# The recurrence's gates as pairs of half-height matmuls

## The chip, the cores and the metric

The kernel runs on one core of a Trainium2 chip. What is compared is the time of one execution in device microseconds (us); for the kernel before it is 1622.69, the median of three runs. The engines are named as in the profile: PE (matmuls) with PEld (its weight loads), DVE (elementwise), ACT (activations by table), POOL and SP (here they mostly issue transfers). SBUF is the memory that the engines work from, with 128 partitions; PSUM holds the matmuls' results, in banks of 128 x 512 numbers.

## The reference

A trunk of two layers over 512 positions with 1024 channels: each layer is a SwiGLU block, a mixer and a second SwiGLU block. The mixer of the first layer is the recurrent one, and only that is changed:

```python
def block_diag_linear(x, w, b):                 # 16 heads of 64 channels
    xh = x.reshape(bsz, s, h, dh)
    return (jnp.einsum('bshi,hij->bshj', xh, w) + b).reshape(bsz, s, h * dh)

def rg_lru(x, w_a, b_a, w_x, b_x, lam):
    gate_a = jax.nn.sigmoid(block_diag_linear(xf, w_a, b_a))
    gate_x = jax.nn.sigmoid(block_diag_linear(xf, w_x, b_x))
    log_a = -LRU_C * gate_a * jax.nn.softplus(-lam)
    a = jnp.exp(log_a)
    mult = jnp.sqrt(-jnp.expm1(2.0 * log_a))
    bx = xf * gate_x * mult
    ...                                         # h[t] = a[t] * h[t-1] + bx[t]

def recurrent_mixer(x, w_in, conv_w, conv_b, ...):
    y, r = jnp.split(x @ w_in, 2, axis=-1)
    r = causal_depthwise_conv(r, conv_w, conv_b)
    return (gelu(y) * rg_lru(r, ...)) @ w_out
```

## The kernel before

The large products are done in blocks of 512 x 512 by a scheme of seven products instead of eight. Every fp32 operand of a product is split into a high and a low part (`split`: ACT makes `hi` by a copy, DVE makes `lo` by a subtraction), and a product is three matmuls, `hi*hi + lo*hi + hi*lo` (`mm3`, L223 to L225).

The work is a list of steps, `subs`. A step is one piece of weight (`raw`, 512 KB, loaded by SP up to eight ahead), its split (`whi` on ACT, `wlo` on DVE, done three steps ahead), and its matmuls. All other work hangs on hooks: `hook(n, phase, fn)` runs `fn` at step `n`, in the phases pre, mid, rest (before the step's matmuls are written down), end and late (behind them). This gives the order in which each engine's instructions stand; each engine takes its own in that order and waits on semaphores for the others'. POOL issues transfers that add a second block of weight to one in SBUF (`raw.add`, L137); it takes its instructions in order too.

In the recurrence (`recurrent`) channels lie on partitions and positions on columns. A group `c` of 128 channels, 0 to 7, is two heads. The input product of `c` gives `r` (a bank of PSUM, 24 matmuls; for c = 0 to 3 the positions come in two halves, because the second half of the normed input is ready later). `r_post(c)` then does, by hooks:

- ACT scales `r` and adds the bias: `rc`. DVE adds the three other taps of the convolution, reading `r` again (`taps`). This ends the use of the bank.
- `rc` is split into `hi` and `lo`.
- `gate`: two block-diagonal weights of 128 x 128, one for a and one for x, each with the two heads' 64 x 64 blocks on the diagonal and zeros elsewhere, give two banks of 128 x 512: 6 matmuls.
- `sigmoids`: ACT makes `g` (a), `g` (x) and from a `tl` (a tanh).
- `product`: DVE multiplies `rc` by the x gate into `pr`.

Behind that come, by `plan`, exponentials of a (groups 0 to 4 together, 5 to 7 together), squares and roots into the factor `tl`, the scan over positions (`scan`), the other half of the input product (y0 to y7, eight more steps), `gelu`, and their product, which is the left side of the output product. The eight banks for products and gates are six (`bank`) in a ring and two others (`aux`). ACT holds one table of functions at a time: sigmoid, exponential, root and gelu each need a load (`ACT_TABLE_LOAD`).

The gates' steps are at `g` = the step of `r` plus 1 or 2, so that gates 3 and 4 follow each other, and 6 and 7.

Of the kernel before, what the change touches and what calls it, by code (L numbers as in the profile page):

```python
# [10 lines left out]
AF = mybir.ActivationFunctionType  # L11
ALU = mybir.AluOpType

P = 128
# [10 lines left out]
V_F1, V_MIX, V_F2, V_CW, V_CB, V_GA, V_GX, V_LAM, V_SB = 0, 16, 32, 48, 80, 88, 96, 104, 112  # L25
# [27 lines left out]
def trunk(ctx: ExitStack, tc: tile.TileContext, a: dict, out: bass.AP):  # L53
    nc = tc.nc
# [12 lines left out]
    def nm(s):  # L67
        uid[0] += 1
        return f"{s}_{uid[0]}"

    def slot(dt=F32, name="s"):
        return sp.tile([P, T], dt, tag="s", name=nm(name))

    def bank(name="ps"):
        return mmp.tile([P, 512], F32, tag="mm", name=nm(name))

    def aux(name="aux"):
        return auxp.tile([P, 512], F32, tag="aux", name=nm(name))
# [4 lines left out]
    def f32(t):  # L83
        return t.bitcast(F32)

    def tt(o, x, y, op):
        nc.vector.tensor_tensor(out=o, in0=x, in1=y, op=op)  # L87
# [4 lines left out]
    def stt(o, x, s, y, op0, op1):  # L92
        nc.vector.scalar_tensor_tensor(out=o, in0=x, scalar=s, in1=y, op0=op0, op1=op1)

    def act(o, x, f, **k):
        nc.scalar.activation(out=o, in_=x, func=f, **k)  # L96

    def split(src):

        w = src.shape[-1]  # L100
        hi, lo = slot(F32R, "hi")[:, :w], slot(F32R, "lo")[:, :w]
        act(hi, src, AF.Copy)
        tt(lo, src, f32(hi), ALU.subtract)
        return hi, lo
# [108 lines left out]
    def hook(n, phase, fn):  # L213


        hooks.setdefault((n, phase), []).append(fn)
# [5 lines left out]
    def mm3(ps, wh, wl, xh, xl, start, stop):  # L222
        nc.tensor.matmul(ps, wh, xh, start=start, stop=False)  # L223
        nc.tensor.matmul(ps, wh, xl, start=False, stop=False)  # L224
        nc.tensor.matmul(ps, wl, xh, start=False, stop=stop)  # L225
# [16 lines left out]
    def vcol(row):  # L242
        return vec[:, row : row + 1]
# [685 lines left out]
    def recurrent(w_in, w_out, norm):  # L929
        gates = {}  # L930

        def load_gates():
            for name in ("a", "x"):
                w = a[f"rec_gate_{name}_w"]
                for q in range(2):
                    g = slot(name="gw")
                    nc.gpsimd.memset(g, 0.0)
                    gv = g.rearrange("p (c j) -> p c j", c=4)
                    wv = w[0, q * 8 : (q + 1) * 8].rearrange("(c two) i j -> two i c j", two=2)
                    for two in range(2):  # L940
                        nc.sync.dma_start(
                            out=gv[two * 64 : (two + 1) * 64, :, two * 64 : (two + 1) * 64], in_=wv[two])
                    gates[name, q] = g

        def split_gate(name, q):
            gates[name, q] = split(gates[name, q])

        at0 = len(subs)
        y0 = at0 + 12
        hook(at0 - 34, "late", load_gates)  # L950
        for n, (name, q) in enumerate((name, q) for q in range(2) for name in ("a", "x")):
            hook(at0 - 26 + 2 * n, "mid", lambda name=name, q=q: split_gate(name, q))

        rc, ga, gx, tl, pr, ym = {}, {}, {}, {}, {}, {}

        def r_post(c, ps):
            n = now[0]
            g = n + (2 if c < 4 or c == 6 else 1)
            v = rc[c] = slot(name="rc")
            hl, pss = [], []  # L960
            act(v, ps, AF.Identity, scale=vcol(V_CW + 24 + c), bias=vcol(V_CB + c))

            def taps():
                for k in (0, 1, 2):
                    stt(v[:, 3 - k :], ps[:, : T - 3 + k], vcol(V_CW + 8 * k + c), v[:, 3 - k :], ALU.mult, ALU.add)

            def gate():
                for name in "ax":
                    pg = bank("gate")
                    wh, wl = gates[name, c // 4]  # L970
                    cs = slice((c % 4) * P, (c % 4 + 1) * P)
                    mm3(pg, wh[:, cs], wl[:, cs], hl[0], hl[1], True, True)
                    pss.append(pg)
                hl.clear()

            def sigmoids():
                for dst, brow in ((ga, V_GA), (gx, V_GX)):
                    dst[c] = slot(name="g")
                    act(dst[c], pss.pop(0), AF.Sigmoid, bias=vcol(brow + c))
                tl[c] = slot(name="tl")  # L980
                act(tl[c], ga[c], AF.Tanh, scale=lru_c[:, c : c + 1])

            def product():
                pr[c] = slot(name="pr")
                tt(pr[c], rc.pop(c), gx.pop(c), ALU.mult)

            hook(n, "late", taps)
            hook(n + 1, "mid", lambda: hl.extend(split(v)))
            hook(g, "end", gate)
            hook(g + 1, "mid", sigmoids)  # L990
            hook(g + 2, "mid", product)

        hh = {}

# [101 lines left out]
        for c in range(4):  # L1096
            again += mk(D + c * P, lambda ps, c=c: r_post(c, ps), True)
        subs.extend(again)
        for c in range(4, KD):
            mk(D + c * P, lambda ps, c=c: r_post(c, ps), False)  # L1100
# [157 lines left out]
    def lru_consts():  # L1258
# [44 lines left out]
        for i in range(13, 0, -2):  # L1303
# [17 lines left out]
    last = FinalNorm()  # L1321
    ffn(a["ffn1_w_in"][0], a["ffn1_w_out"][0], TileNorm(V_MIX))
    recurrent(a["rec_w_in"][0], a["rec_w_out"][0], BlockNorm(V_F2))
    ffn(a["ffn2_w_in"][0], a["ffn2_w_out"][0], BlockNorm(V_F1 + 8))
    ffn(a["ffn1_w_in"][1], a["ffn1_w_out"][1], BlockNorm(V_MIX + 8, True))
# [7 lines left out]

    stage = slot(name="stage")
    rows = [(a["ffn1_norm"], V_F1, 16), (a["mix_norm"], V_MIX, 16), (a["ffn2_norm"], V_F2, 16),
            (a["rec_conv_w"][0], V_CW, 32), (a["rec_conv_b"], V_CB, 8), (a["rec_gate_a_b"], V_GA, 8),
            (a["rec_gate_x_b"], V_GX, 8), (a["rec_lambda"], V_LAM, 8), (a["sg_b_s"][0], V_SB, 8)]
    first_gain = tp.tile([8, P], F32, tag="fgain1", name="first_gain", bufs=1)
    nc.scalar.dma_start(out=first_gain, in_=a["ffn1_norm"][0].rearrange("(n p) -> n p", p=P))

# [33 lines left out]
    ps = aux("vec")  # L1374
# [3 lines left out]
    def vec_rest():  # L1378
        for src, r0, n in rows:
            flat = src.rearrange("h d -> (h d)") if len(src.shape) == 2 else src.rearrange("o h d -> (o h d)")  # L1380
            nc.gpsimd.dma_start(out=stage[r0 : r0 + n, :P], in_=flat.rearrange("(n p) -> n p", p=P))

    def vec_rest_t():
        ps = aux("vec")
        nc.tensor.transpose(ps[:, :V_ROWS], stage[:V_ROWS, :P], ident[:V_ROWS, :V_ROWS])
        opening["vec"] = ps

    first = BlockNorm(V_F1)
# [31 lines left out]
    for n, phase, fn in ((0, "late", vec_rest),  # L1420
                         (2, "pre", lambda: (subs[2].split(True), parts(0, "A11"), parts(1, "A11"))),
                         (2, "pre", lambda: (subs[3].split(), value(0, "A11", True), value(1, "A11", True))),
                         (2, "end", lambda: (turn(0, "A22", bank), turn(1, "A22", bank))),
                         (3, "pre", lambda: (parts(0, "A22"), parts(1, "A22"))),
                         (3, "mid", lambda: (value(0, "A22"), value(1, "A22", True))),
                         (3, "end", lambda: (turn(0, "A21"), turn(1, "A21"))),
                         (4, "mid", lambda: (parts(0, "A21"), parts(1, "A21"))),
                         (4, "rest", lambda: (value(0, "A21"), value(1, "A21")))):
        hook(n, phase, fn)
# [57 lines left out]
```

## Time and profile before

| | |
|---|---|
| median of 3 runs | 1622.69 us (1622.64 to 1623.0) |
| the profiled execution, its own time | 1622.86 us |
| its span in the profile | 1621.2 us |
| PE, DVE, ACT busy | 99%, 85%, 64% of the span |
| the recurrence's input products and gates | about 343 to 445 us of the span |
| all 48 gate matmuls | 366.1 to 407.2 us of the span, with other products between them |

The span runs from the first to the last instruction of one execution; the rows that the prediction shows are of this execution, and their times count from its start.

### The profile page before, as it was taken

To read this page: it belongs to the slowest core of one execution; us is meant where nothing else is said; L and a number is where in the kernel's file an instruction comes from. 1 tells how busy PE (TensorE), PEld (TensorE's weight loads), DVE (VectorE), ACT (ScalarE), POOL (GpSimd) and SP (SyncE) were. 2 spreads that over 40 slices of the span, in tenths; PEclk is the share of its full clock that TensorE was granted. 3 is DMA by queue.
4 is the path that set the end of the run, shared out by engine and by line. 5 is a ranking of instruction groups with operands and counts; after the bars stand their busy time and mean duration, and the time that the engine had idled before them with its cause. 6 is when DMAs were issued, how large, how long until landed. Compare 5 with 4: busy or idle time off the path is not lost.

```text
span 1621.2 us, 20840 instructions
## 1 busy us (share of the span) xinstructions
PE 1608.2 (99%) x7451; PEld 1327.0 (82%) x7451; DVE 1373.8 (85%) x1839; ACT 1036.8 (64%) x1504; POOL 221.8 (14%) x201
## 2 busy tenths in 40 slices
PE   9999999999999999999999999999999999999998
PEld 7888888888888888888888888888888788888886
DVE  6898888888998787877887978878978988879778
ACT  7656556658776556556775565566886766565665
POOL 2111111100010111111101111111211011111110
PEclk9999999999999999999999999999999999999999
DMA  9776876943383786876838768768877557686693
GB/s 275 183 168 166 210 179 158 214 126 105 92 208 86 176 217 156 209 168 158 206 86 192 168 162 212 181 154 208 217 192 191 155 120 192 167 208 159 161 206 100
DMA packets 164695, 279.29 MB, mean 172 GB/s; under 512 B 11520, under 2 KB 38000, under 8 KB 164592
## 3 DMA queue, kind: packets, MB, share of 16 engines
q1 hardware_dynamic: 115088, 184.84, 36.2%
q0 software_dynamic: 47712, 91.30, 33.8%
q10 hardware_dynamic: 1792, 1.84, 0.4%
q8 instruction: 58, 0.95, 0.2%
q14 instruction: 45, 0.37, 0.1%
HBM read 275.84 MB, written 2.10 MB: 171 GB/s over the span
## 4 chain that ended last, share of the span: by engine, by line
PE 94%; DVE 2%; ACT 2%; issue 1%; DMA 0%; SPq 0%; DVEq 0%; ACTq 0%
PE A L365 14%; PE A L366 14%; PE A L367 14%; PE C L366 7%; PE C L367 7%; PE C L365 7%; PE p L751 5%; PE B L365 4%; PE B L367 4%; PE B L366 4%; PE e L265 3%; PE r L225 2%; PE r L223 2%; PE r L224 2%; PE Q L367 1%; PE Q L365 1%
## 5 line engine op out<-in xcount | busy, mean ns | idle before, releaser
L96 ACT ACTIVATE whi<-raw 128x1024 fp32r<-128x1024 f32 (+1 forms) x536 | 553.2, 1033 | 388.0 <-PE A L366 103.9
L87 DVE TENSOR_TENSOR wlo<-raw,whi 128x1024 fp32r<-128x1024 f32 (+1 forms) x537 | 639.7, 1194 | 181.6 <-ACT whi L96 180.3
L365 PE MATMUL A<-whi,hi 128*128 128x512 f32 x1016 | 404.1, 398 | 0.0
L367 PE MATMUL A<-wlo,hi 128*128 128x512 f32 x1016 | 396.9, 391 | 0.0
L366 PE MATMUL A<-whi,lo 128*128 128x512 f32 x1016 | 396.5, 390 | 0.0
L367 PEld LDWEIGHTS A<-wlo,hi 128*128 128x128 f32 x1016 | 190.8, 188 | 41.6 <-DVE wlo L87 0.3
L366 PEld LDWEIGHTS A<-whi,lo 128*128 128x128 f32 x1016 | 191.1, 188 | 38.6 <-DVE lo L87 0.8
L365 PEld LDWEIGHTS A<-whi,hi 128*128 128x128 f32 x1016 | 190.9, 188 | 37.5
L366 PE MATMUL C<-whi,lo 128*128 128x512 f32 x560 | 218.7, 391 | 0.9 <-DVE lo L87 0.8
L365 PE MATMUL C<-whi,hi 128*128 128x512 f32 x560 | 218.5, 390 | 0.0
L367 PE MATMUL C<-wlo,hi 128*128 128x512 f32 x560 | 218.1, 389 | 0.0
L137 POOL DMA_DIRECT2D raw<-in_ffn_w_in_dram x82 | 98.8, 1205 | 741.1 <-DVE raw L87 524.5
L137 POOL DMA_DIRECT2D raw<-in_ffn_w_out_dram x72 | 83.0, 1160 | 378.7 <-DVE wlo L87 148.7
L87 DVE TENSOR_TENSOR raw<-raw,raw 128x1024 f32<-128x1024 f32 (+1 forms) x108 | 129.7, 1201 | 1.1 <-DMA raw<-in_ffn_w_out_dram 0.6
L87 DVE TENSOR_TENSOR lo<-a,hi 128x512 fp32r<-128x512 f32 (+1 forms) x188 | 123.1, 663 | 3.7 <-ACT hi L96 3.3
L366 PEld LDWEIGHTS C<-whi,lo 128*128 128x128 f32 x560 | 105.1, 188 | 24.7 <-DVE lo L87 3.2
L96 ACT ACTIVATE hi<-a 128x512 fp32r<-128x512 f32 (+1 forms) x188 | 112.4, 601 | 17.5 <-DVE a L87 14.3
L365 PEld LDWEIGHTS C<-whi,hi 128*128 128x128 f32 x560 | 105.2, 188 | 21.8
L367 PEld LDWEIGHTS C<-wlo,hi 128*128 128x128 f32 x560 | 105.2, 188 | 21.7
L96 ACT ACTIVATE c<-A 128x512 f32<-128x512 f32 x132 | 77.4, 594 | 56.3 <-PE A L367 55.9
L365 PE MATMUL B<-whi,hi 128*128 128x512 f32 x280 | 112.1, 400 | 0.0
L367 PE MATMUL B<-wlo,hi 128*128 128x512 f32 x280 | 109.4, 391 | 0.0
(161 smaller groups left out, 2106.3 us busy)
## 6 DMA issues: line engine op xcount, KB each, us to landing
raw<-in_ffn_w_in_dram SPq DMA_DIRECT2D x162, 512.0 KB, 4.4
raw<-in_ffn_w_out_dram SPq DMA_DIRECT2D x100, 512.0 KB, 5.3
raw<-in_ffn_w_in_dram POOLq DMA_DIRECT2D x82, 512.0 KB, 7.5
raw<-in_ffn_w_out_dram POOLq DMA_DIRECT2D x60, 512.0 KB, 8.1
raw<-in_sg_w_in_dram SPq DMA_DIRECT2D x20, 512.0 KB, 6.4
raw<-in_rec_w_in_dram SPq DMA_DIRECT2D x16, 512.0 KB, 3.8
raw<-in_ffn_w_in_dram SPq DMA_DIRECT2D x30, 256.0 KB, 5.0
raw<-in_sg_w_in_dram POOLq DMA_DIRECT2D x12, 512.0 KB, 7.8
```

What stands on the lines that cost most here:

```text
L87: nc.vector.tensor_tensor(out=o, in0=x, in1=y, op=op)
L96: nc.scalar.activation(out=o, in_=x, func=f, **k)
L137: nc.gpsimd.dma_start(out=self.v, in_=src, accum_op=ALU.add)
L223: nc.tensor.matmul(ps, wh, xh, start=start, stop=False)
L224: nc.tensor.matmul(ps, wh, xl, start=False, stop=False)
L225: nc.tensor.matmul(ps, wl, xh, start=False, stop=stop)
L265: nc.tensor.transpose(ps[:, o : o + P], src(q, s), ident)
L365: nc.tensor.matmul(ps, zh, wh, start=fresh and i == 0, stop=False, **k)
L366: nc.tensor.matmul(ps, zl, wh, start=False, stop=False, **k)
L367: nc.tensor.matmul(ps, zh, wl, start=False, stop=end, **k)
L751: nc.tensor.matmul(bank_of(half, s), z, (sub.lo if m == 2 else sub.hi)[:, q, :], start=left[2] == "2" and (h, q, m) == (0, 0, 0), stop=lef ...
```

## The change

It does the gates with the two heads apart. A group's weights are now one tile of 128 x 128: in the rows of the first head stand its a columns and then its x columns, in the rows of the second head its x columns and then its a columns, and no zeros. The first head's matmul takes rows 0 to 63 of weight and input, the second's rows 64 to 127, each into a bank of its own, and they are written down in turn: 3 pairs of half-height matmuls per group in place of 6 full ones. The first bank then holds a of the first head above its x, the second x of the second head above its a. So a lies where it belongs, and x is in the other half of the partitions.

The sigmoids' results are put together in one of two ways:

- groups 0, 1, 2 and 5 (`MOVED`): two sigmoids of 128 partitions, and three transfers of 64 x 512 from SBUF to SBUF, issued by POOL: two make the x gate, the third puts the second head's a into its place in `ga`, over what the first transfer reads. The tanh has a hook of its own, later.
- groups 3, 4, 6 and 7: four sigmoids of 64 partitions, which put a in its place, and two transfers for the x gate.

With this the products `pr` of groups 0 to 2 are a step later, gate 5 is a step later (behind r7 instead of r6), the gate weights are two tiles instead of four (two splits less, no clearing by POOL), and the two biases are loaded in four pieces instead of two rows of blocks.

```diff
         def load_gates():
-            for name in ("a", "x"):
-                w = a[f"rec_gate_{name}_w"]
-                for q in range(2):
-                    g = slot(name="gw")
-                    nc.gpsimd.memset(g, 0.0)
-                    gv = g.rearrange("p (c j) -> p c j", c=4)
-                    wv = w[0, q * 8 : (q + 1) * 8].rearrange("(c two) i j -> two i c j", two=2)
-                    for two in range(2):
-                        nc.sync.dma_start(
-                            out=gv[two * 64 : (two + 1) * 64, :, two * 64 : (two + 1) * 64], in_=wv[two])
-                    gates[name, q] = g
+            for q in range(2):
+                g = slot(name="gw")
+                gv = g.rearrange("p (c j) -> p c j", c=4)
+                for two, names in enumerate(("ax", "xa")):
+                    for k, name in enumerate(names):
+                        wv = a[f"rec_gate_{name}_w"][0, q * 8 : (q + 1) * 8].rearrange("(c two) i j -> two i c j", two=2)
+                        nc.sync.dma_start(out=gv[two * H2 : (two + 1) * H2, :, k * H2 : (k + 1) * H2], in_=wv[two])
+                gates[q] = g
...
-        for n, (name, q) in enumerate((name, q) for q in range(2) for name in ("a", "x")):
-            hook(at0 - 26 + 2 * n, "mid", lambda name=name, q=q: split_gate(name, q))
+        for q in range(2):
+            hook(at0 - 24 + 4 * q, "mid", lambda q=q: split_gate(q))
+        HALVES = slice(0, H2), slice(H2, P)
+        MOVED = (0, 1, 2, 5)
 
         def r_post(c, ps):
             n = now[0]
-            g = n + (2 if c < 4 or c == 6 else 1)
+            g = n + (1 if c in (4, 7) else 2)
...
             def gate():
-                for name in "ax":
-                    pg = bank("gate")
-                    wh, wl = gates[name, c // 4]
-                    cs = slice((c % 4) * P, (c % 4 + 1) * P)
-                    mm3(pg, wh[:, cs], wl[:, cs], hl[0], hl[1], True, True)
-                    pss.append(pg)
+                pss.extend(bank("gate") for _ in range(2))
+                w = gates[c // 4]
+                cs = slice((c % 4) * P, (c % 4 + 1) * P)
+                for m in range(3):
+                    for ps, r in zip(pss, HALVES):
+                        nc.tensor.matmul(ps, w[m == 2][r, cs], hl[m == 1][r, :], start=m == 0, stop=m == 2)
                 hl.clear()
 
             def sigmoids():
-                for dst, brow in ((ga, V_GA), (gx, V_GX)):
-                    dst[c] = slot(name="g")
-                    act(dst[c], pss.pop(0), AF.Sigmoid, bias=vcol(brow + c))
+                p0, p1 = pss
+                pss.clear()
+                if c in MOVED:
+                    ga[c], u = slot(name="g"), slot(name="gu")
+                    act(ga[c], p0, AF.Sigmoid, bias=vcol(V_GA + c))
+                    act(u, p1, AF.Sigmoid, bias=vcol(V_GX + c))
+                    swap(c, ga[c][HALVES[1], :], u[HALVES[0], :])
+                    nc.gpsimd.dma_start(out=ga[c][HALVES[1], :], in_=u[HALVES[1], :])
+                    return
+                ga[c], u = slot(name="g"), slot(name="gu")
+                for dst, ps, brow, r in ((ga[c], p0, V_GA, 0), (ga[c], p1, V_GX, 1), (u, p0, V_GA, 1), (u, p1, V_GX, 0)):
+                    r = HALVES[r]
+                    act(dst[r, :], ps[r, :], AF.Sigmoid, bias=vcol(brow + c)[r, :])
+                swap(c, u[HALVES[1], :], u[HALVES[0], :])
+                tanh()
+
+            def swap(c, first, second):
+                gx[c] = slot(name="gx")
+                for r, src in zip(HALVES, (first, second)):
+                    nc.gpsimd.dma_start(out=gx[c][r, :], in_=src)
+
+            def tanh():
                 tl[c] = slot(name="tl")
                 act(tl[c], ga[c], AF.Tanh, scale=lru_c[:, c : c + 1])
...
             hook(g, "end", gate)
             hook(g + 1, "mid", sigmoids)
-            hook(g + 2, "mid", product)
+            if c in MOVED:
+                hook(g + (2 if c in (2, 5) else 3), "mid", tanh)
+            hook(g + (3 if c < 3 else 2), "mid", product)
...
-            (a["rec_conv_w"][0], V_CW, 32), (a["rec_conv_b"], V_CB, 8), (a["rec_gate_a_b"], V_GA, 8),
-            (a["rec_gate_x_b"], V_GX, 8), (a["rec_lambda"], V_LAM, 8), (a["sg_b_s"][0], V_SB, 8)]
+            (a["rec_conv_w"][0], V_CW, 32), (a["rec_conv_b"], V_CB, 8), (a["rec_lambda"], V_LAM, 8),
+            (a["sg_b_s"][0], V_SB, 8)]
...
+        for two, (names, r0) in enumerate((("ax", V_GA), ("xa", V_GX))):
+            for k, name in enumerate(names):
+                src = a[f"rec_gate_{name}_b"][0].rearrange("(c two) d -> two c d", two=2)[two]
+                nc.gpsimd.dma_start(out=stage[r0 : r0 + 8, k * P // 2 : (k + 1) * P // 2], in_=src)
```

More of the change, by code (lines that the diff above doesn't have):

```diff
@@ L930, in recurrent, with split_gate @@
         gates = {}
+        H2 = P // 2
         def load_gates():
-            for name in ("a", "x"):
-                w = a[f"rec_gate_{name}_w"]
-                for q in range(2):
-                    g = slot(name="gw")
-                    nc.gpsimd.memset(g, 0.0)
-                    gv = g.rearrange("p (c j) -> p c j", c=4)
-                    wv = w[0, q * 8 : (q + 1) * 8].rearrange("(c two) i j -> two i c j", two=2)
-                    for two in range(2):
-                        nc.sync.dma_start(
-                            out=gv[two * 64 : (two + 1) * 64, :, two * 64 : (two + 1) * 64], in_=wv[two])
-                    gates[name, q] = g
-        def split_gate(name, q):
-            gates[name, q] = split(gates[name, q])
+            for q in range(2):
[6 more added lines that the diff above has]
+                gates[q] = g
+        def split_gate(q):
+            gates[q] = split(gates[q])
         at0 = len(subs)
```

## The prediction

> **What bounds the kernel now.** I read the first part of the page, then its chain of what ended last, and then the timeline of each engine over the recurrence.
>
> ```profile
> span 1621.2 us, 20840 instructions
> PE 1608.2 (99%) x7451; PEld 1327.0 (82%) x7451; DVE 1373.8 (85%) x1839; ACT 1036.8 (64%) x1504; POOL 221.8 (14%) x201
> PE 94%; DVE 2%; ACT 2%; issue 1%; DMA 0%; SPq 0%; DVEq 0%; ACTq 0%
> ```
>
> Over the whole span TensorE (PE) sets the time: 99% busy, and 94% of the chain. On that average alone, time taken off PE comes off the span. But the gates stand in a stretch of their own, so I read that stretch on PE first. In a timeline row: start, length, engine, line, operation and, at the end in brackets, the idle time before it.
>
> ```profile
> 366.07 0.40 PE L223 MATMUL gate<-hi,hi 128*128 128x512 f32 x1
> 367.46 0.28 PE L223 MATMUL r<-zh,whi 128*128 128x256 f32 x1
> 371.72 0.47 PE L223 MATMUL r<-zh,whi 128*128 128x512 f32 x1
> 405.83 0.39 PE L223 MATMUL gate<-hi,hi 128*128 128x512 f32 x1
> 406.06 0.39 PE L224 MATMUL gate<-lo,hi 128*128 128x512 f32 x1
> 407.19 0.39 PE L223 MATMUL r<-zh,whi 128*128 128x512 f32 x1
> 434.39 0.39 PE L223 MATMUL r<-zh,whi 128*128 128x512 f32 x1
> 434.84 0.39 PE L225 MATMUL r<-zh,wlo 128*128 128x512 f32 x1
> ```
>
> Names: r0 to r7 are the eight products that feed the convolution, gate 0 to gate 7 theirs, y0 to y7 the products after r7. The first two rows are gate 0: six matmuls in 1.39 us, 0.23 each (started every 0.23, each 0.40 long, so they overlap). Rows 3, 4 and 6 are r4, the start of gate 7, and y1. y1 to y5 take 434.39 - 407.19 = 27.20, 5.44 each; the last two rows are y6's first and third matmuls. Now the engines that feed the gates, ACT and then DVE, over the same time:
>
> ```profile
> 379.10 1.26 ACT L96 ACTIVATE g<-gate,vec 128x512 f32<-128x512 f32 x2
> 380.24 0.72 ACT L96 ACTIVATE tl<-g,lru_c 128x512 f32<-128x512 f32 x1
> 384.27 0.78 ACT L96 ACTIVATE rc<-r,vec 128x512 f32<-128x512 f32 x1 [2.36 <-PE r L225]
> 384.95 1.05 ACT L96 ACTIVATE whi<-raw 128x1024 fp32r<-128x1024 f32 x1
> 385.90 1.26 ACT L96 ACTIVATE g<-gate,vec 128x512 f32<-128x512 f32 x2
> 388.79 0.74 ACT L96 ACTIVATE tl<-g,lru_c 128x512 f32<-128x512 f32 x1
> 389.40 0.65 ACT L96 ACTIVATE hi<-rc 128x512 fp32r<-128x512 f32 x1
> 394.45 0.76 ACT L96 ACTIVATE rc<-r,vec 128x512 f32<-128x512 f32 x1
> 396.18 1.28 ACT L96 ACT_TABLE_LOAD   x1
> 397.47 1.27 ACT L96 ACTIVATE g<-gate,vec 128x512 f32<-128x512 f32 x2
> 402.98 0.63 ACT L96 ACTIVATE hi<-rc 128x512 fp32r<-128x512 f32 x1 [1.50 <-DVE rc L93]
> 417.09 1.95 ACT L96 ACTIVATE g<-g,lru_nc 128x512 f32<-128x512 f32 x3
> ```
> ```profile
> 369.26 2.31 DVE L93 SCALAR_TENSOR_TENSOR rc<-r,vec,rc 128x509 f32<-128x509 f32 x3
> 395.24 2.32 DVE L93 SCALAR_TENSOR_TENSOR rc<-r,vec,rc 128x509 f32<-128x509 f32 x3 [0.38 <-ACT rc L96]
> 404.54 0.69 DVE L87 TENSOR_TENSOR lo<-rc,hi 128x512 fp32r<-128x512 f32 x1
> 419.49 0.67 DVE L87 TENSOR_TENSOR a<-g 128x512 f32<-128x512 f32 x1
> 431.35 1.20 DVE L87 TENSOR_TENSOR wlo<-raw,whi 128x1024 fp32r<-128x1024 f32 x1
> ```
>
> ```profile
> 385.00:390.00 5.00, 5.00 (x24) 4.14 (x23) 3.98 (x5) 5.00 (x9) 0.00 (x0) 1.00 0.14 27
> 390.00:395.00 5.00, 5.00 (x24) 4.14 (x23) 3.37 (x5) 4.97 (x8) 1.20 (x1) 1.00 0.32 106
> ```
>
> Here PE is not alone. In the last two rows, windows of 5 us, the columns are PE, PEld, DVE, ACT: after its wait for r5 (2.36) ACT is as full as PE, 5.00 and 4.97 of 5, from 384.27 to rc(6) at 394.45. DVE has no idle time between the taps of rc(6), 395.24, and the lower part of rc(7), 404.54 to 405.23. Gate 7's second matmul, which reads that part, starts at 406.06: a margin of 0.83 us. Later DVE's lower weights for y6 end at 432.55, and y6's third matmul starts at 434.84: a margin of 2.29. So the chain rc, taps, hi, lo runs less than a microsecond ahead of PE; the 94% doesn't show it.
>
> **PE's own part.** 48 matmuls of 128 rows become 48 of 64 rows in 24 pairs. If both halves run at once a pair takes 0.23, and 24 x 0.23 = 5.5 us leave PE, 0.69 per gate; if in turn, none. I take at once. No row shows two halves together; the only matmul on few rows is an eight-row one:
>
> ```profile
> 3.50 0.27 PE L1375 MATMUL vec<-ident,first_gain 8*128 8x8 f32 x1
> 3.81 1.12 PE L265 MATMUL e<-ident,x 128*128 128x128 f32 x4
> ```
>
> The next full matmul follows it by 0.31. The gates stand in six stretches (3 with 4, 6 with 7 together), so there are twelve changes between half and whole; each costs between 0 and 0.40 - 0.23 = 0.17, the tail of one matmul, not more than 2.0 in all. The page of the Trainium skill "TensorEngine Tiling (Array Packing)", section "Key Properties", says that a change of tiling mode drains the engine; by it the upper end, 2.0, would hold, and what PE saves would be 3.5.
>
> Gates 0 and 1 give nothing in any case. Six banks hold r0 to r3 and gate 0; gate 1 takes those of r0 and r1, and r4 that of r2. r2's last reader is its taps on DVE, which end at 369.26 + 2.31 = 371.57, and r4 starts at 371.72, its second matmul 0.31 later. PE gets there 1.4 us earlier and waits. DVE's work before that is unchanged.
>
> **ACT's part, up to gate 7.** From rc(5) on: r5 ends 0.69 earlier (gate 2), so rc(5) starts at 383.6. Up to rc(6) ACT had 384.27 to 394.45 = 10.18 of work. Added: tanh(1) and tanh(2), which move here from behind their sigmoids, 2 x 0.61 (388.79 to 389.40) = 1.22; and the sigmoids of 3 and 4 in halves, eight for four. No row of ACT has fewer than 128 partitions. Each half covers the same 512 columns, so I take the whole one's spacing, 1.26 - 0.69 = 0.57, as its cost: 4 x 0.57 = 2.3; that a half costs less is rival 1. Then a wait: tanh(2) needs the third transfer of c=2, which overwrites what the first one reads, so POOL issues it only after the first has landed.
>
> ```profile
> out_dram<-x SPq DMA_DIRECT2D x2, 128.0 KB, 2.4
> raw<-in_ffn_w_out_dram POOLq DMA_DIRECT2D x12, 256.0 KB, 4.7
> stage<-in_ffn_norm_dram POOLq DMA_DIRECT2D x2, 8.0 KB, 3.3
> 5.68 0.50 POOL L1381 DMA_DIRECT2D stage<-in_sg_b_s_dram  x1
> 392.89 1.20 POOL L137 DMA_DIRECT2D raw<-in_rec_w_out_dram  x1 [73.34 <-DVE a L87]
> ```
>
> The last figure of the first three is issue to landing. A swap moves 128 KB between SBUF tiles; no such transfer is in the trace. Bounds: 2.4 (same size, SP's queue) and 4.7 (POOL, twice the size, adding). I take POOL's own shortest, 3.3. With tanh(0) now ahead of it, the first sigmoid of 2 ends at about 379.10 + 0.61 + 0.69 = 380.4; the first transfer lands at 383.7, the third at 387.0. ACT reaches tanh(2) at 383.6 + 0.68 + 0.95 + 0.61 = 385.8: a wait of 1.2, between 0 and 4.0. Behind it on ACT stand the sigmoids of 3 and 4, hi(5), five exponentials and rc(6). So rc(6) starts at 383.6 + 10.18 + 1.22 + 2.3 + 1.2 = 398.5, 4.05 late. The page "DMA: Bandwidth & Descriptors" of the Trainium skill, section "Anatomy of one DMA — SWDGE (gpsimd) path", fits 2.0 us plus bytes over 436 GB/s; its estimate is 2.3, by which tanh(2) doesn't wait and the final sum is 1.2 less.
>
> DVE's chain from the taps of rc(6) to lo(7) holds the same work as before and no slack, so lo(7) ends at 405.23 + 4.05 = 409.3 and the second pair of gate 7 starts there, not at 406.06: 3.2 late. Gate 7 is 0.69 shorter: PE leaves it 2.5 us later than before. Everything saved in gates 2 to 6 is waited away here.
>
> **After gate 7.** hi(7) waits for its taps, which come 4.05 late too: 407.0. From hi(7) to the exponentials of 5 to 7 ACT had 417.09 - 402.98 = 14.1. Added: four more half sigmoids 2.3, tanh(5) 0.61, and one table load more, 1.28 (a lone tanh after the roots gets one table, the sigmoids behind it another). They start at 407.0 + 14.1 + 4.2 = 425.3, 8.2 late. DVE's squares followed the exponentials' start by 419.49 - 417.09 = 2.40, because it still had scans; now it has none left and starts after one exponential, 0.7. From there to the end of y6's lower weights it had 432.55 - 419.49 = 13.06: 425.3 + 0.7 + 13.1 = 439.1. PE wants them at 434.84 + 2.5 = 437.3: a wait of 1.8, 4.3 in all.
>
> ```profile
> 440.00:450.00 10.00, 10.00 (x45) 8.28 (x45) 10.00 (x17) 7.34 (x11) 2.41 (x2) 1.00 0.66 131
> 450.00:460.00 10.00, 10.00 (x45) 8.26 (x44) 10.00 (x15) 6.33 (x8) 3.61 (x3) 1.00 1.03 242
> ```
>
> In these windows (PE, PEld, DVE, ACT) DVE is busy 10.00 of 10, so its lateness isn't made up at once: I add 1, between 0 and 2.
>
> At no cost: two splits and four POOL memsets less, two bias transfers of 0.50 more (all before 300 us, beside a full PE); 20 swaps on POOL at 0.5 to 1.2 each. The addition into `rec_w_out`, issued at 392.89, moves behind those of c=4, to about 395; its weights are used after 445.
>
> **Sum.** 4.3 + 1 = 5.3 more on the profiled execution (span 1621.2, its own time 1622.86, 0.17 over the median 1622.69): 1628.0 against the median. With landings of 2.4 it is 1.2 less, and without the last term another 1.0: 1625.8. With 4.7 and 2 at the end, 2.8 + 1 more: 1631.8; transfers crowded by loads may add 2.
>
> **Rivals.** 1: *halves are half the work.* If a 64-row sigmoid takes half of 0.57, the 2.3 fall away at both places: rc(6) is 1.75 late, lo(7) ends at 407.0, PE leaves gate 7 0.2 late, the exponentials start at 404.7 + 14.1 + 0.61 + 1.28 = 420.7, and y6's weights, at 434.5, are in time; with the last term +1.2, 1623.9. For it: no row shows a 64-row activation. Against: the cost goes with columns in every ACT row above. 2: *PE decides after all*, faster: gates 2 to 7 give 6 x 0.69 = 4.1, and no wait follows, 1618.6. Its place is gate 7: its second pair would start at 406.06 - 5 x 0.69 = 402.6, so lo(7) has to end 2.6 earlier than now, and rc(6) to start by 391.8. For it: PE's 99%. Against: ACT has no idle time to give up there, and the two tanh alone add 1.22. By the rule of the Trainium skill's tiling page this gain is 2.0 smaller. 3: *the halves run in turn*, so the change doesn't do what it says: rc(5) stays at 384.27, the later steps come 0.69 later, gate 7 isn't shorter and ends 3.9 late, y6 waits 1.1: 3.9 + 1.1 + 1 = 6.0, 1628.7, little more, since PE waits anyway.
>
> **Numbers.** Forecast 0.62, halves in turn 0.10, half-cost sigmoids 0.18, PE decides 0.10. Faster 0.10, within 0.2% (3.2 us, about what can be told from no change) 0.18, slower 0.72. The range goes from 1620.0, short of rival 2, to 1635.0; the forecast's own is 1625.5 to 1634.
>
> **What would show it.** Right: pairs of gate matmuls 0.23 apart; PE idle before the gate matmuls of c=7 (2 us or more, released by ACT or DVE) and before y6; ACT idle at tanh(2) on a DMA; one table load more; half sigmoids of 0.69. Wrong: no idle on PE between 395 and 445, half sigmoids of about 0.35, swaps landing in 2 us, or rc(6) no later than 394.5.

## The result, and the profile after

The changed kernel takes 1628.78 us (median of 6 runs, 1628.04 to 1629.44), the kernel before beside it 1622.95 (6 runs, 1622.64 to 1623.08): ratio 1.0036, 95% interval [1.0026, 1.0046], 5.8 us more. The forecast was 1628.0. The profiled execution of the changed kernel took 1628.05 us. Of its page, the lines that answer to those of before:

```profile
span 1626.4 us, 20908 instructions
PE 1608.1 (99%) x7451; PEld 1322.5 (81%) x7451; DVE 1372.5 (84%) x1837; ACT 1042.5 (64%) x1511; POOL 232.0 (14%) x219
PE 88%; DVE 6%; ACT 4%; issue 1%; DMA 0%; SPq 0%; DVEq 0%; ACTq 0%
```

PE's busy time is the same to 0.1 us, so the sum shows nothing. The chain does: 94% on PE has become 88%, and DVE and ACT have 10% of it. The view of waits on PE, 360 to 470 us of the span (line, for whom, us in total, times, longest), says where:

```profile
PE gate L978 <- ACT hi L96: 2.2, 1, 2.2
PE gate L978 <- DVE lo L87: 1.8, 2, 1.3
PE r L223 <- DVE rc L93: 0.6, 1, 0.6
PE C L366 <- DVE lo L87: 0.6, 1, 0.6
PE r L225 <- DVE wlo L87: 0.4, 1, 0.4
```

The rows are the five longest. The same view of the kernel before has no row. `C` is a bank of the output product. The timeline of PE has these waits in order; 64*128 with x2 is a pair, two halves that start together:

```profile
370.73 0.47 PE L223 MATMUL r<-zh,whi 128*128 128x512 f32 x1 [0.63 <-DVE rc L93]
382.59 0.39 PE L225 MATMUL r<-zh,wlo 128*128 128x512 f32 x1
382.91 0.50 PE L978 MATMUL gate<-hi,hi 64*128 64x512 f32 x2
383.24 0.40 PE L978 MATMUL gate<-lo,hi 64*128 64x512 f32 x2
383.48 0.40 PE L978 MATMUL gate<-hi,lo 64*128 64x512 f32 x2
...
384.50 0.50 PE L223 MATMUL r<-zh,whi 128*128 128x512 f32 x1
384.83 0.40 PE L224 MATMUL r<-zl,whi 128*128 128x512 f32 x1
406.89 0.51 PE L978 MATMUL gate<-hi,hi 64*128 64x512 f32 x2 [2.22 <-ACT hi L96]
407.90 0.61 PE L978 MATMUL gate<-lo,hi 64*128 64x512 f32 x2 [0.51 <-DVE lo L87]
408.87 0.80 PE L223 MATMUL r<-zh,whi 128*128 128x512 f32 x1
438.47 0.50 PE L225 MATMUL r<-zh,wlo 128*128 128x512 f32 x1 [0.38 <-DVE wlo L87]
461.47 0.49 PE L366 MATMUL C<-whi,lo 128*128 128x512 f32 x1 [0.57 <-DVE lo L87]
```

The first row is r4. It waits for DVE, whose work up to there is unchanged, and starts 0.99 earlier than in the profile before (371.72). This execution had gained 0.99 within the first 25 us of the kernel, far ahead of the change, so a lateness below is a start in its profile less the start before, plus 0.99. For other kernels the same is done with their own r4. y1 (408.87) is 2.7 late, y6's third matmul (438.47) 4.6, the matmul in `C` that waits for its lower part (461.47; 456.38 before) 6.1, and nothing is won back behind it.

The last place in the kernel before, first DVE's lower part and then the matmul that reads it:

```profile
454.85 0.70 DVE L87 TENSOR_TENSOR lo<-a,hi 128x512 fp32r<-128x512 f32 x1
456.38 0.39 PE L366 MATMUL C<-whi,lo 128*128 128x512 f32 x1
```

The lower part ended at 455.55, 0.83 ahead of the matmul. Now the timeline of ACT in the changed kernel and then that of DVE:

```profile
383.01 0.78 ACT L96 ACTIVATE rc<-r,vec 128x512 f32<-128x512 f32 x1 [2.54 <-PE r L225]
384.64 1.32 ACT L96 ACTIVATE tl<-g,lru_c 128x512 f32<-128x512 f32 x2
385.87 1.38 ACT L96 ACTIVATE g<-gate,vec 64x512 f32<-64x512 f32 x2
397.24 0.76 ACT L96 ACTIVATE rc<-r,vec 128x512 f32<-128x512 f32 x1
406.21 0.63 ACT L96 ACTIVATE hi<-rc 128x512 fp32r<-128x512 f32 x1 [0.94 <-DVE rc L93]
413.47 1.28 ACT L96 ACT_TABLE_LOAD   x1
414.76 0.73 ACT L96 ACTIVATE tl<-g,lru_c 128x512 f32<-128x512 f32 x1
415.51 1.28 ACT L96 ACT_TABLE_LOAD   x1
424.59 1.95 ACT L96 ACTIVATE g<-g,lru_nc 128x512 f32<-128x512 f32 x3
```
```profile
407.17 0.68 DVE L87 TENSOR_TENSOR lo<-rc,hi 128x512 fp32r<-128x512 f32 x1
425.35 0.69 DVE L87 TENSOR_TENSOR a<-g 128x512 f32<-128x512 f32 x1 [2.47 <-ACT g L96]
437.22 1.20 DVE L87 TENSOR_TENSOR wlo<-raw,whi 128x1024 fp32r<-128x1024 f32 x1
460.73 0.68 DVE L87 TENSOR_TENSOR lo<-a,hi 128x512 fp32r<-128x512 f32 x1
```

Two half sigmoids in a row (x2) last 1.38, and the next pair starts 1.29 behind (387.16): 0.645 for each half of 64 rows, no less than the 0.57 of a whole one of 128. The lone tanh(5) stands between two table loads. The exponentials of 5 to 7 start at 424.59, 8.5 late, and DVE stands idle for 2.47 until the first of them is done. The transfers (last figure: issue to landing) are these:

```profile
gx<-gu POOLq DMA_DIRECT2D x12, 128.0 KB, 2.3
gx<-g POOLq DMA_DIRECT2D x4, 128.0 KB, 2.3
g<-gu POOLq DMA_DIRECT2D x4, 128.0 KB, 3.0
```

And one thing that the prediction doesn't have. In these two windows the seventh figure is the granted clock of PE:

```profile
404.74:408.16 3.42, 0.76 (x4) 0.44 (x6) 3.38 (x5) 2.45 (x4) 1.59 (x3) 1.00 0.33 78
408.16:411.57 3.41, 3.41 (x10) 2.19 (x9) 3.31 (x6) 2.31 (x4) 0.00 (x0) 0.50 0.61 195
```

From 408.16 to 411.57 the clock is at half, behind a window in which PE was busy for 0.76 of 3.42 us, and y1's first matmuls start 0.43 apart instead of 0.23. Half of 3.41 is 1.7 us of PE's time.

### The profile page after: what moved, and what is told of

It is laid out like the page before. It is cut to its first block, busy times and chain, and to the rows that moved or that the text cites. A ratio compares the mean times of both kernels' runs of the same rounds, so it can differ in the third digit from the quotient of the medians.

```text
span 1626.4 us, 20908 instructions
## 1 busy us (share of the span) xinstructions
PE 1608.1 (99%) x7451; PEld 1322.5 (81%) x7451; DVE 1372.5 (84%) x1837; ACT 1042.5 (64%) x1511; POOL 232.0 (14%) x219
## 4 chain that ended last, share of the span: by engine, by line
PE 88%; DVE 6%; ACT 4%; issue 1%; DMA 0%; SPq 0%; DVEq 0%; ACTq 0%
PE A L365 14%; PE A L366 14%; PE A L367 14%; PE C L366 7%; PE C L367 7%; PE C L365 7%; PE p L751 5%; PE B L365 4%; PE B L367 4%; PE B L366 4%; PE e L265 3%; DVE wlo L87 1%; PE Q L365 1%; PE Q L367 1%; PE Q L366 1%
```

## The experiments

Each time is a median beside runs of the kernel before on the same chip (1622.8 to 1623.05 in all of them). The theory is the prediction's: TensorE saves little, what the change adds on ScalarE makes gate 7 and the exponentials of 5 to 7 late, and VectorE carries that to the output product.

**x1_pairs.** The step list of the kernel before, with the pairs:

```diff
-        MOVED = (0, 1, 2, 5)
+        MOVED = ()
...
-            g = n + (1 if c in (4, 7) else 2)
+            g = n + (2 if c < 4 or c == 6 else 1)
...
-                for dst, ps, brow, r in ((ga[c], p0, V_GA, 0), (ga[c], p1, V_GX, 1), (u, p0, V_GA, 1), (u, p1, V_GX, 0)):
-                    r = HALVES[r]
-                    act(dst[r, :], ps[r, :], AF.Sigmoid, bias=vcol(brow + c)[r, :])
-                swap(c, u[HALVES[1], :], u[HALVES[0], :])
+                for dst, ps, brow in ((ga[c], p0, V_GA), (u, p1, V_GX)):
+                    act(dst, ps, AF.Sigmoid, bias=vcol(brow + c))
+                gx[c] = u
...
-            hook(g + (3 if c < 3 else 2), "mid", product)
+            hook(g + 2, "mid", product)
```

> The pairs alone: order and steps of the kernel before, every gate's sigmoids whole on its two banks, tanh at once, no transfers. It leaves out the putting together of the halves (the x gate and the second head's a stay in the half where the product leaves them). Theory (TensorE saves little, the scalar engine's additions cost): gates 2 to 5 save 1.4 us together, as in the trace of the changed kernel; rc(5) then starts 0.3 earlier, and with it lo(7), at 404.9 instead of 405.2, so gate 7's second pair waits about 0.8 and y1 starts 1.5 to 1.9 earlier; no half clock, no wait at y6: 1621.2 us (1620.4 to 1622.0), 1.7 below the kernel before. Rival, the halves or their mode changes cost more than they save: 1623 or more. Rival, TensorE decides after all: gates 2 to 7 give the full 4.1, 1618.8.

Measured: 1621.96 against 1623.05, ratio 0.9994 [0.9986, 1.0003]. y1 starts 1.5 earlier; gate 7 waits for `lo` as expected:

```profile
404.80 0.50 PE L978 MATMUL gate<-lo,hi 64*128 64x512 f32 x2 [0.67 <-DVE lo L87]
```

1.1 us lower where 1.7 were expected, and the interval takes in no change. y1 is 1.5 early, but `C` only 1.0: it waits there for its lower part, which comes only 0.2 earlier. That PE decides (1618.8) is out. So even with the halves put together for nothing, the pairs would be worth about a microsecond in this order, if anything.

**x2_whole.** Whole sigmoids in groups 3, 4, 6 and 7:

```diff
-                for dst, ps, brow, r in ((ga[c], p0, V_GA, 0), (ga[c], p1, V_GX, 1), (u, p0, V_GA, 1), (u, p1, V_GX, 0)):
-                    r = HALVES[r]
-                    act(dst[r, :], ps[r, :], AF.Sigmoid, bias=vcol(brow + c)[r, :])
+                for dst, ps, brow in ((ga[c], p0, V_GA), (u, p1, V_GX)):
+                    act(dst, ps, AF.Sigmoid, bias=vcol(brow + c))
```

> The changed kernel with two whole sigmoids of 128 rows in place of four of 64 rows in groups 3, 4, 6 and 7; transfers stay. It leaves out moving the second head's a of these four groups to its place. Theory (half sigmoids are the price): 4 x 0.645 - 2 x 0.57 = 1.4 us less per group, so rc(6) and lo(7) come 2.8 earlier, TensorE's waits at gates 6 and 7 fall from 4.0 to about 1 to 1.5, the clock is not halved, y6 doesn't wait: 4 to 5.5 us below the changed kernel, 1623.3 to 1624.8. Rival, the price is elsewhere (transfers, the two moved tanh, the later gate 5): less than 2 below it, 1627 or more.

Measured: 1623.90, ratio 1.0006 [0.9997, 1.0015], 4.9 us below the changed kernel. PE's two waits at gate 7 are these, the clock stays at 1.00, and the exponentials of 5 to 7 start at 419.51 instead of 424.59:

```profile
404.65 0.50 PE L978 MATMUL gate<-hi,hi 64*128 64x512 f32 x2 [0.96 <-ACT hi L96]
405.65 0.50 PE L978 MATMUL gate<-lo,hi 64*128 64x512 f32 x2 [0.51 <-DVE lo L87]
```

`C` is 0.7 late, where it is 6.1 late in the changed kernel. Eight sigmoids more on an engine that is busy 64% of the span are most of the loss.

**x3_no_transfers.** The changed kernel with `gx[c] = u` in place of the swaps.

> The changed kernel without its 20 swaps: half sigmoids and the later tanh stay as they are, the x gate is read where the sigmoids leave it. It leaves out putting the halves together. Theory (the transfers are hidden; ACT's two tanh had no idle time before them): within 0.5 us of the changed kernel, 1628.3 to 1629.3. Rival, transfers cost (a wait of tanh, products or the addition into rec_w_out that POOL issues behind them): 1.5 us or more below it.

Measured: 1628.86, ratio 1.0037 [1.0025, 1.0050]: the transfers cost nothing, as the theory says. In its trace the clock of PE is halved for 6.83 us, twice as long as in the changed kernel, and `C` is 6.1 late as there.

**x4_in_turn.** The loops exchanged:

```diff
-                for m in range(3):
-                    for ps, r in zip(pss, HALVES):
+                for ps, r in zip(pss, HALVES):
+                    for m in range(3):
```

> The changed kernel with the two halves written in turn: three matmuls of the first head, then three of the second. Theory (neighbours in the queue overlap only where one is in each half): a gate has five starts of 0.23 instead of three, 0.45 more; that is waited for anyway in gates 0 to 2 and partly in 3 to 5, and shows once in rc(5) and once in gate 7: 0.5 to 1.3 us above the changed kernel, and matmuls of one half 0.23 apart in the trace. Rival, the order in the queue doesn't matter (each half has its own): within 0.3 of it.

Measured: 1629.04, ratio 1.0036 [1.0024, 1.0049], 0.3 above the changed kernel: the rival holds. Where nothing waits, the trace has the same pairs, x2 and 0.23 apart, in gates 0 to 5. The theory was wrong on this: the three matmuls of the second head, written behind the first head's, start with them. Only a wait keeps them back, as in gate 6:

```profile
403.26 0.50 PE L978 MATMUL gate<-hi,hi 64*128 64x512 f32 x1
405.05 0.50 PE L978 MATMUL gate<-lo,hi 64*128 64x512 f32 x1 [1.30 <-DVE lo L87]
405.06 0.50 PE L978 MATMUL gate<-hi,hi 64*128 64x512 f32 x1
```

The second head's first matmul (405.06) needs nothing that is missing, but stands behind the first head's second.

**x5_fill.** Twelve matmuls for nothing, to keep PE busy:

```diff
                 w = gates[c // 4]
+                for _ in range({6: 4, 7: 8}.get(c, 0)):
+                    nc.tensor.matmul(pss[0], w[0][:, :P], S.z[0][0], start=True, stop=True)
```

> The changed kernel with twelve full matmuls of gate weight by normed input added, whose result nobody reads (four ahead of gate 6, eight ahead of gate 7, each 128x512, 0.23 started to start, into the gate's own bank, which the gate's first matmul then clears). They fill the 1.29 and 2.22 us in which TensorE waits there. Theory (the clock was halved because TensorE was mostly idle from 402 to 408): no half clock behind gate 7, y1's matmuls 0.23 apart again, 1.0 to 1.8 us below the changed kernel, though it does more work: 1627.4 (1626.9 to 1627.9). Rival, the half clock has another cause (transfers, the change of form, the other engines): it stays, and the time is that of the changed kernel or up to 0.7 above.

Measured: 1629.37, ratio 1.0042 [1.0029, 1.0054]. The clock isn't halved any more, so PE's idling was the cause, and y1's matmuls (409.97, 410.20) are 0.23 apart. Yet the time is 0.6 higher, not 1.0 to 1.8 lower:

```profile
405.66 2.14 PE L976 MATMUL gate<-zh,hi 128*128 128x512 f32 x8
439.54 0.50 PE L225 MATMUL r<-zh,wlo 128*128 128x512 f32 x1 [1.96 <-DVE wlo L87]
```

The last row is the answer: y6's wait, 0.38 in the changed kernel, is 1.96 here. The half clock only made PE arrive later at a weight that wasn't ready. In the traces `C` is 6.1 late in the one and 6.2 in the other; the 0.6 between the medians of two sets of runs has no row that explains it. My theory had the cause right and the price wrong.

**x7_gate5.** Gate 5 back behind r6 (`g = n + 1` for c = 5).

> The changed kernel with one step moved back: gate 5 behind r6 instead of r7, so that its sigmoids and its tanh come in the sigmoids' table that groups 3 and 4 use, or one load for all. Theory (the lone tanh among the roots costs a table load of 1.28 and 0.6 to 0.7 of tanh, on the path to the exponentials of 5 to 7): one table load less, these exponentials 1.9 earlier, y6 doesn't wait and the output product waits less; gate 5 now waits 2 to 3 us for lo(5), which comes off the waits of gates 6 and 7: 0.8 to 2.2 us below the changed kernel, 1627.3. Rival, only gate 7 counts: within 0.4 of it.

Measured: 1628.20, ratio 1.0033 [1.0020, 1.0045], 0.6 below the changed kernel, less than the theory's 0.8 and more than the rival's 0.4. One load less, but the exponentials of 5 to 7 come only 1.0 earlier (at 424.08, with r4 at 371.22), not 1.9:

```profile
407.40 0.72 ACT L96 ACTIVATE tl<-g,lru_c 128x512 f32<-128x512 f32 x1 [3.26 <-DMA g<-gu]
424.08 1.95 ACT L96 ACTIVATE g<-g,lru_nc 128x512 f32<-128x512 f32 x3
460.97 0.50 PE L366 MATMUL C<-whi,lo 128*128 128x512 f32 x1 [0.57 <-DVE lo L87]
```

Now tanh(5) waits 3.26 for its third transfer, with hi(7) behind it. The wait that the prediction feared at tanh(2) exists, in another place: the extra table load had bought its absence.

**x6_order and x8_before_exp_later.** A whole kernel in another order, and as a control the kernel before with the last line alone. The code is shortened: `g` is written out, and the line that puts tanh(3) where tanh(2) stands, two steps behind its gate, is left out.

```diff
+        MOVED = (0, 1, 2, 3, 5)                      # was (0, 1, 2, 5)
+            g = n + (1 if c in (4, 5, 7) else 2)     # gate 5 behind r6
+            hook(g + 1, "rest" if c == 4 else "mid", sigmoids)
-        plan(-2, "rest", (exp_, 0, 1, 2, 3, 4), (oma2, 0, 1))
+        plan(-1, "rest", (exp_, 0, 1, 2, 3, 4), (oma2, 0, 1))
```

> A whole kernel with the pairs, in another order around them: group 3 also takes two whole sigmoids and the three transfers; gate 5 stands behind r6 as in the kernel before, its tanh in the sigmoids' table; group 4's sigmoids come behind hi(5); the exponentials of groups 0 to 4 come behind rc(6) instead of ahead of it. Theory (the scalar engine's chain from rc(5) to rc(6) is what gate 7 waits for): rc(6) no longer stands behind 3.2 us of exponentials and a table load, half sigmoids are left in groups 4, 6 and 7, gate 7 waits 1.5 at most, no half clock: 1621.5 us (1620.4 to 1622.8), 0.2 to 2.6 below the kernel before. Rival, the squares and scans, which come later by this, make y6 or the output product late: 1624 or more.

> A control: the kernel before with one thing changed, the exponentials of groups 0 to 4 (and the first two squares) behind rc(6) instead of ahead of it, as in x6_order. No pairs. Theory (here TensorE waits for nothing in the recurrence, gate 7 has a margin of 0.83): within 0.5 us of the kernel before. Rival, this order alone brings what x6_order brings: 1.5 or more below it.

Measured: 1625.12, ratio 1.0014 [1.0005, 1.0022], and 1623.63, ratio 1.0003 [0.9994, 1.0012]. The order takes 3.7 us off the changed kernel and still doesn't reach the kernel before: the rival's time (1624 or more) holds. Its reason doesn't: behind its scans DVE stands idle for 1.04 until the first exponential of 5 to 7 is done, so these make the output product late, not the squares and scans. Gate 7 waits less, the half clock is gone, and `C` comes as ever 36.9 behind them:

```profile
421.51 1.95 ACT L96 ACTIVATE g<-g,lru_nc 128x512 f32<-128x512 f32 x3
458.39 0.50 PE L366 MATMUL C<-whi,lo 128*128 128x512 f32 x1 [0.58 <-DVE lo L87]
```

The control is 0.65 above the kernel before beside it, a little more than the 0.5 expected, and its interval takes in no change.

**What sets the end.** From the start of these exponentials to the matmul in `C` that waits for `lo` it is 461.47 - 424.59 = 36.88 in the changed kernel, 36.88 in x3 and x6, 36.89 in x4, x5 and x7. PE reaches that place by quite different ways, with the clock halved for 0 to 6.83 us, with y6 waiting 0 to 2 us, and always waits there 0.57 or 0.58. In x2, whose exponentials come early enough to find DVE still at its scans, it is 37.13. In x9 and x12 below, which have another chain on DVE because POOL takes products, it is 36.7 and 37.1. In the kernel before it is 456.38 - 417.09 = 39.29, and PE doesn't wait. So the end follows the exponentials of 5 to 7, as soon as these are more than 39.29 - 36.88 = 2.4 late: 8.5 late gives 6.1.

**x9_pool_products, x10_order_pool, x11_before_pool.** To relieve VectorE, five products go to POOL, in the changed kernel, in x6_order and in the kernel before:

```diff
-                tt(pr[c], rc.pop(c), gx.pop(c), ALU.mult)
+                (nc.gpsimd if c >= 3 else nc.vector).tensor_tensor(out=pr[c], in0=rc.pop(c), in1=gx.pop(c), op=ALU.mult)
```

> The changed kernel with one kind of work moved from VectorE to POOL: the products of rc and the x gate of groups 3 to 7 (five of 128x512, 0.60 to 0.69 each on VectorE), three of which stand on VectorE right ahead of lo(6), the taps of rc(7) and lo(7). Theory (what sets the end behind gate 7 is VectorE's chain: lo(7), then from the exponentials of 5 to 7 on without idle time to the output product): VectorE gets 1.8 us back ahead of lo(7) and 1.2 more ahead of y6 and the output product, TensorE's waits (4.5 at the gates, 0.4 and the hidden part at y6, 0.9 at the output product) shrink by 2 to 3 us: 1626.2 (1625.3 to 1627.0). Rival, POOL is too slow or its queue, where the products stand among the swaps and wait for them, delays the next swaps: 1628.3 or more.

> x6_order with the products of groups 3 to 7 on POOL as in x9_pool_products. Theory (in x6_order too VectorE's chain is late, 2.5 us of waits at gate 7 and 0.9 at the output product): 1.2 to 2.5 below x6_order: 1623.2 (1622.4 to 1624.0), which is the kernel before or a little less. Rival, in x6_order gate 7 waits for rc(7) on ScalarE behind the exponentials, which this doesn't move: within 0.7 of 1625.1.

> A control: the kernel before with the products of groups 3 to 7 on POOL, nothing else. Theory (its TensorE waits for nothing here, so relief on VectorE is worth nothing): within 0.6 us of the kernel before. Rival, the relief is worth something by itself: 1.5 or more below it.

Measured: 1629.33, ratio 1.0038 [1.0023, 1.0052]; 1624.47, ratio 1.0016 [1.0007, 1.0025]; 1623.15, ratio 1.0001 [0.9992, 1.0010]. In the changed kernel this brings nothing (0.5 above it; the rival's time). In x6_order it brings 0.65, within the rival's 0.7, and in the kernel before nothing that stands out. POOL and DVE in x9:

```profile
394.66 3.07 POOL L1009 TENSOR_TENSOR pr<-rc,gx 128x512 f32<-128x512 f32 x2 [1.16 <-DVE lo L87]
396.61 1.66 DVE L93 SCALAR_TENSOR_TENSOR tl<-a,tl 128x512 f32<-128x512 f32 x1
398.91 0.69 DVE L93 SCALAR_TENSOR_TENSOR tl<-a,tl 128x512 f32<-128x512 f32 x1
```

The same DVE instruction takes 0.69 alone and 1.66 while POOL multiplies: it ends 0.5 behind POOL's second product. Three of these instructions in x9 are lengthened so, by 1.0 each, against five products of 0.6 that DVE is spared. PE does leave gate 7 a microsecond earlier than in the changed kernel (y1 is 1.7 late instead of 2.7). But ACT's roots wait 1.5 for the second of them, the exponentials of 5 to 7 come 8.8 late instead of 8.5, and `C` 6.2. The page "SBUF — State Buffer" of the Trainium skill, section "SBUF: two separate sides", has a rule for it: VectorE with two inputs in SBUF and GpSimd reading SBUF lock each other out for a whole instruction. The rows agree.

**x12_order_pool_fill.** x10_order_pool with four such matmuls ahead of gate 7, because its clock is halved behind it (for 3.41 us) and nothing there waits.

> x10_order_pool with four full matmuls of gate weight by normed input ahead of gate 7, whose result nobody reads (0.91 and two changes of form, inside the 1.16 that gate 7 waits there). In x10_order_pool TensorE waits for nothing behind gate 7, and its clock is halved for 3.4 us there. Theory (the halving comes from TensorE's two waits at gate 7 and is paid in full where nothing behind it waits): no half clock, 1.5 below x10_order_pool: 1623.0 (1622.4 to 1623.7). Rival, with 0.5 us of wait left in gate 7 the clock is halved all the same, or the halving has another cause: within 0.5 of 1624.5.

Measured: 1624.32, ratio 1.0011 [1.0002, 1.0020], 0.15 below x10 where 1.5 were expected; both spread too widely (1623.4 to 1626.9, x10 1623.7 to 1629.4) for 0.15 to tell anything. The clock is 1.00 throughout the stretch, so the theory's cause holds again, and its price fails again: now y6 waits 0.15 and `C` 0.58, where x10 had neither wait; both kernels are 1.6 late at `C`. No whole version tried beats the kernel before.

## Why the prediction was right, point by point

The time (1628.0 against 1628.78), the sign and the mechanism held. The time alone would not have told the forecast from rival 3 (1628.7); the rows do. The steps, as lateness against the kernel before:

| step | predicted | measured |
|---|---|---|
| rc(5) | -0.67 | 383.01 + 0.99 - 384.27 = -0.3 |
| rc(6) | +4.05 | 397.24 + 0.99 - 394.45 = +3.8 |
| lo(7) ends | 409.3 | 407.85 + 0.99 = 408.8 |
| PE leaves gate 7 (y1) | +2.5 | 408.87 + 0.99 - 407.19 = +2.7 |
| exponentials of 5 to 7 | 425.3 | 424.59 + 0.99 = 425.6 |
| y6's lower weights end | 439.1 | 438.42 + 0.99 = 439.4 |
| y6's third matmul | +4.3 | +4.6 |
| last term | 1 (0 to 2) | 6.1 - 4.6 = 1.5 |

**PE's own part.** At once, as taken: pairs 0.23 apart. The mode changes: from 382.59 to 384.83 are eight starts, 1.82 at 0.227 each, and took 2.24, so 0.42 for two changes; gate 2's two, from 376.04 to 377.58, cost 1.54 - 5 x 0.227 = 0.40. That is 0.2 each, over the bound of 0.17 that the tail of one matmul was to give, and the reason why rc(5) gained 0.3 and not 0.67. The term had been left out of the sum; at 0.41 for each of six stretches PE would save 5.5 - 2.5 = 3.0 (an estimate from these rows) and not 5.5. The rule of the Trainium skill's page "TensorEngine Tiling (Array Packing)", section "Key Properties", by which a change of mode drains the engine, agrees with a cost at every change. Gates 0 and 1 gave nothing: r4 waits 0.63 for `rc` on DVE.

**The half sigmoids** were the largest term up to rc(6) and were undersized: 0.645 each, so 8 x 0.645 - 4 x 0.57 = 2.9 in each of the two places instead of 2.3. x2_whole shows that they carry the loss: 4.9 us go with them. Rival 1 is out.

**The wait of tanh(2)** (1.2, at bounds 0 to 4.0) wasn't there: 384.64 starts both tanh without a gap, and x3_no_transfers shows no price at all. The step that failed is the landing, 3.3 from a POOL load: the first two swaps land in 2.3, where the estimate by the Trainium skill's page "DMA: Bandwidth & Descriptors", section "Anatomy of one DMA — SWDGE (gpsimd) path", had them. The third lands in 3.0; that of c = 2, issued at 382.17, took 2.9, and was there about 0.2 before ACT reached its tanh.

That rc(6) came out so near is luck: rc(5) 0.4 later and the halves 0.6 dearer than in the sum stand against the 1.2 of the wait that wasn't (-0.3 + 1.2 + 2.9 = 3.8, where -0.67 + 1.22 + 2.3 + 1.2 = 4.05 was forecast).

**From hi(7) on**, 4.2 more were counted and 18.38 - 14.11 = 4.3 came: halves 0.6 dearer, the roots waiting a little less. The extra table load is there. x7_gate5 shows that taking it away wins little, since another wait stands behind it.

**The last term** was a guess, 1 between 0 and 2, and measured 1.5. The trace of the kernel before had it: the lower weights of y6 came 2.29 ahead of PE, the lower part for `C` (454.85 to 455.55, matmul at 456.38) only 0.83. DVE is as late at the one as at the other (437.22 against 431.35 and 460.73 against 454.85, 6.9 with the 0.99), so PE is held there for 2.29 - 0.83 = 1.46 more.

**Not in the prediction**: the half clock. It cost 1.7 us of PE's time and, by x3_no_transfers, x5_fill and x12_order_pool_fill, nothing that lasts of the kernel's, because y6 and `C` wait for DVE without it. Then the chain reads as predicted: y6's wait was forecast as 1.8 and is 1.96 in x5_fill. So the agreement at the end isn't luck, as it is in part at rc(6): the chain that the prediction followed, ACT to DVE, is the one that sets the end.

**Rivals 2 and 3.** PE doesn't decide: with the halves put together for nothing x1_pairs gains 1.1 (between 2.3 less and 0.5 more time), not 4.1. The halves do run at once, and x4_in_turn shows that this isn't even a matter of the order in which they are written.

What stays open is whether a finer order could make the pairs pay: by x1_pairs there would be about 1 us to win, if anything, and none of the three orders tried (x6, x7, and the change itself) gets there.

## What to carry to other kernels

An engine at 99% isn't a bound where another engine's chain runs less than a microsecond ahead of it: find the margins in the stretch that is changed, and count what the change adds to that other engine, instruction by instruction, before counting what it takes off the busy one. To find which chain sets an end, look for the interval that stays constant over several variants (here 36.88 to 36.89 us from the exponentials to the output product); a loss that doesn't change it, such as a halved clock ahead of a wait, is free, and to mend it wins nothing.

## What the runs showed of the hardware that was not expected

- The clock of PE fell to 0.50 for 3.41 us after a stretch in which PE wasn't idle throughout: from 404.74 to 408.16 it worked for 0.76 us, in short bursts. In every trace the stretches at full and at half clock last whole multiples of 3.413 us, up to the last fall at the end of the kernel: 402.77 is 118 of them, 1611.09 is 472, and at half it is one in the changed kernel, x7, x9 and x10 and two in x3 and x4. So it seems to count where the waits lie on this grid. With waits of 1.16 and 0.51 in gate 7 the clock fell in x10_order_pool, whose waits share one window; with 1.37 and 1.11 it stayed in x6_order, where they fall into two. The figures behind each window are again length, PE, PEld, DVE, ACT, POOL and clock:

```profile
404.26:407.67 3.41, 1.87 (x9) 1.10 (x10) 3.38 (x6) 3.04 (x5) 0.00 (x0) 1.00 0.94 178
402.32:405.73 3.41, 2.04 (x11) 0.86 (x10) 3.34 (x5) 2.51 (x4) 0.00 (x0) 1.00 0.79 125
405.73:409.14 3.41, 2.30 (x13) 1.66 (x12) 3.34 (x6) 2.55 (x4) 0.00 (x0) 1.00 0.65 185
```

  The first row is of x10, the others are of x6. What the limit is stays open: in x5_fill a window with PE busy 1.51 of 3.41 (436.07 to 439.48), at y6's wait, is not followed by half clock. The page "TensorE: Matmul & The Clock Gate" of the Trainium skill, section "What's actually happening", has a free-running window of 3.4 us; the trace agrees with its length. Its table asks for an idle window before the clock falls; here windows with PE busy for 0.76 to 1.87 us were enough.
- A change between whole and half-height matmuls costs PE about 0.2 us (0.42 and 0.40 for two).
- Matmuls on the two halves of the rows overlap also when three of one half are written ahead of three of the other (x4_in_turn: pairs 0.23 apart). A wait of one half holds the other, if it stands behind it.
- A sigmoid on 64 partitions takes no less time than one on 128 (0.645 against 0.57 from start to start).
- A product on POOL lengthens the VectorE instruction beside it from 0.69 to 1.66 (x9_pool_products).
